# One-layer encoder trunk: the values of all heads projected 512 columns wide in the first stage, and query tiles 0 to 2 as one unit of attention

## The chip, the cores and the metric

The kernel runs on one core of one Trainium2 chip. The metric is the device time of one execution in microseconds (us). Three runs of the kernel before gave 1123.44, 1124.37 and 1125.34 us, so the median is 1124.37 us. All traces are of one profiled execution of that core.

## The reference, cut to what matters

One layer on 1024 tokens of width 1024: RMSNorm and one input projection, whose 2048 columns are 512 of a pooling mixer and 512 each of queries, keys and values; attention of eight heads of 64, where each chunk of 64 tokens sees itself and the eight chunks before it; an output projection; then a gated MLP with a causal convolution, a per-layer embedding and a last norm. The change touches the input projection and the attention alone:

```python
z = hn @ w_in[i]
u = z[..., :POOL_W]
q, k, v = jnp.split(z[..., POOL_W:], 3, axis=-1)
a = pool_mixer(u, pool_w[i], pool_b[i], pool_scale[i])
o = chunk_attention(q, k, v, rel_bias[i])
```

with, for a chunk of queries, `s = q·k * scale + bias`, masked before the first token, `softmax(s)` and `pr·v`.

## The kernel before, in words

**Products.** Everything is computed in float32 with operands split in two: a high half (`hi`, a copy in fp32r made by ScalarE, called ACT here) and a low half (`lo`, the source less `hi`, made by VectorE, called DVE, for some weight blocks by GpSimd, called POOL). `mm3` (L133 to L137) writes one product as three matmuls, hi·hi, hi·lo and lo·hi, so the lines L135, L136 and L137 stand for nearly all of TensorE's (PE's) work. A "product" below is one matmul of these. PE's order is written out by hand; in the attention ACT's and DVE's are too, by `push(t, fn)` with a due time in the unit and `flush()`, which emits what is pending in the order of due times.

**First stage (L230 to L344).** For each of the eight blocks k of the model width, SP loads x in two halves of 512 tokens (L233), the weights of the first pair of query and key heads (L240) and of the values (L237). ACT and DVE weight and split x (L244, L245) and split the weights (`split`, L140 and L141), and square x for the norm (L226, L228). PE multiplies: `start_mm` makes 12 products of 512 columns per k, and `start_v`, one k behind, 9 products of the value columns for the token tiles 0 to 2. Here only the **first four heads' values** are made: 256 columns. `v_tile` makes the same for token tiles 3 to 7, and `v_out` scales and splits the result into `V`.

**Attention (L357 to L751).** A unit is a pair of heads c and one query tile of 128 tokens, except that tiles 0 and 1 make one unit: 7 units for each of 4 pairs, `PER` = 7. `unit(u)` does this in turn: `probs_t(u-1)` transposes the probabilities of the unit before into PSUM (L419); `scores(u)` makes this unit's scores (L396); `ROOM[u % PER]` grants a number of filling steps, each a few products of later projections, drawn from the generator `rest()`; and where a group of query tiles ends, `values` multiplies probabilities and `V` (L471). `softmax` gives DVE the sum with the bias and its minimum (L364, L368), ACT the exponential (L376), DVE the reciprocal (L378), and the scaling of head x = 0 to DVE (L374), of x = 1 to ACT (L372). `probs_out` takes the transposed probabilities out of PSUM as `hi` on ACT (L437) and `lo` on DVE (L439); those past the eighth block of 64 columns lie in other banks and are the "far" ones, with a due time of 3.5 instead of 0.

**Filling.** `rest()` projects the later query, key and mixer columns, 16 steps of three products each per block of 128 columns, and in between (`project_v`, L556) the **other four heads' values**, 256 columns wide, in 32 steps of six products. `weights` and `v_weights` load and split their operands while the block before runs (L502 on ACT, L500 on DVE or POOL); `qk_out` takes a block out of PSUM (L280); `lay` splits it into keys or queries (L309 to L313). `load_bias` loads a head's bias, ACT negates it (L352), POOL writes its two corners (L353, L354). When the units are done, what is left of `rest()` runs beside the output projection.

```python
while credit >= 1:
    if valued[0] and credit < 2 and 4.7 < at[0] < 5.4:
        break
    now[0] += STEP
    credit -= 1
    if next(fill, True) is False:
        break
    lay_due(u)
```

Of the kernel before, what the change touches and what calls it, by code (L numbers as in the profile page):

```python
# [6 lines left out]
F32 = mybir.dt.float32  # L7
# [4 lines left out]
P = 128  # L12
# [52 lines left out]
ROOM = (5.5, 6, 5.5, 6.5, 6.5, 5, 7)  # L65
# [8 lines left out]
UNITS = [(c, ts) for c in range(N_HEADS // 2) for ts in [(0, 1)] + [(t,) for t in range(2, NTOK)]]  # L74
# [26 lines left out]
def trunk(tc, xT, pT, vecs, w_qk0, w_in, w_v, bias, counts, pool_w, w_out, w_up, w_down,  # L101
# [4 lines left out]
    with tc.tile_pool(name="sb", bufs=1) as sb, \  # L106
# [4 lines left out]
        small = sb.tile([P, 88], F32, name="small")  # L111
        R = sb.tile([P, 32768], F32R, name="R")
        F = sb.tile([P, 15488], F32, name="F")
# [56 lines left out]
        biasb = [f(b, 640) for b in (12, 14.5, 57.875)]  # L170
        Sb = [f(b, 640) for b in (17, 19.5)]
# [5 lines left out]
        temps = [f(57.875, 272), f(58.9375, 272)]  # L177
        otmp = f(56.375, 384)
# [16 lines left out]
        wv1 = [r(b, 2048).rearrange("p (k c) -> p k c", k=KT) for b in (128, 136)]  # L195
        VT0 = 3

        def v_mm(t, k, ps, wv):
# [13 lines left out]
        def start_v(k):  # L212
            for t in range(VT0):
                v_mm(t, k, v_ps(t), wv1)
# [15 lines left out]
        for k in range(KT):  # L230
            xs = xraw[k]
            for h in range(2):
# [3 lines left out]
                if k % 2 and h:  # L236
                    sp.dma_start(wvraw[k // 2], w_v[0, :, (k - 1) * 256:(k + 1) * 256])  # L237
# [28 lines left out]
        def v_outs(t, half, ps):  # L266
            s = rstd_tok[:, t:t + 1]
            pv = ps.rearrange("p (h c) -> p h c", h=4)
            hs = slice(4 * half, 4 * half + 4)
            hi, lo = V[:, t, hs, 0:HD], V[:, t, hs, HD:2 * HD]  # L270
            return (lambda: act.activation(hi, pv, AF.Copy, scale=s),
                    lambda: dve.scalar_tensor_tensor(lo, pv, s, rv(hi), ALU.mult, ALU.subtract))

        def v_out(t, half, ps):
            for fn in v_outs(t, half, ps):
                fn()
# [53 lines left out]
        def v_tile(t):  # L330
            for k in range(KT):
                v_mm(t, k, v_ps(t), wv1)

        for t in range(VT0):
            v_out(t, 0, v_ps(t))
        for t in range(VT0, NTOK):
            if t < VT0 + 2:
                rstd_rows(t - VT0)
            v_tile(t)
            v_out(t, 0, v_ps(t))  # L340
# [16 lines left out]
        def softmax(todo, valued):  # L357

            for i, (x, b, ps, S, s_) in enumerate(todo):
# [18 lines left out]
                push(max(2.95 + 0.01 * z, 1.91 + 0.85 * z) if valued else 2.95 + 0.55 * z, lambda s_=s_: dve.reciprocal(s_[:, 2:3], s_[:, 1:2]))  # L378
                push(3.9 + 0.1 * z if x else 3.0 + (0.01 if valued else 0.55) * z, scaled)

        halves = [slice(HD * x, HD * x + HD) for x in range(2)]

        def scores(u):
# [4 lines left out]
            for z, t in enumerate(ts):  # L388
# [3 lines left out]
                places = [[4 + x + 2 * (z + y) for y in range(2 if nk > 3 else 1)] for x in range(2)]  # L392
                for i, (q, k) in enumerate(((Q[0], Kh), (Q[0], Kl), (Q[1], Kh))):
                    for y in range(len(places[0])):
                        for x in range(2):
                            pe.matmul(PS[:, places[x][y], 0:wide], q[halves[x], t * P:(t + 1) * P],  # L396
                                      k[halves[x], ki + y * wide:ki + (y + 1) * wide], start=i == 0, stop=i == 2,
                                      tile_position=(HD * x, 0))
                for x in range(2):
                    p0 = places[x][0]  # L400
                    ps = PS[:, p0:p0 + 3:2, 0:wide] if nk > 3 else PS[:, p0, 0:n]
                    todo.append((x, biasb[(2 * c + x) % 3][:, 640 - n:640], ps, Sb[x][:, z * P:z * P + n],
                                 st[(4 * u + 2 * z + x) % 8]))
            return todo

        def probs_t(u):
# [15 lines left out]
            for t in ts:  # L422
                nk = min(t + 1, BANDT)
                b0 = block_at(t + 1 - nk, t)
                for a, b in ((0, min(nk, 4)), (4, nk)):
# [17 lines left out]
        def values(u):  # L443
# [6 lines left out]
            while c_ >= 2 and len(v_ready) < t1 or u < NU - 1 and at[0] < 2.3:  # L450
# [32 lines left out]
        blocks_, ready = [8 + 1, 4 + 1, 8 + 2, 4 + 2, 8 + 3, None, 4 + 3, 2, 3, 0, 1], {}  # L483

        wvr, wv2, there = [], [], set()
# [9 lines left out]
        def split_later(parts, soon=False):  # L495

            t = now[0] - 0.3 if soon else max(5.2, now[0] + 0.4)
            for i, (name, src, hi, lo) in enumerate(parts):
# [3 lines left out]
                push(t + 0.7 * i * (not soon), lambda src=src, hi=hi: act.activation(hi, src, AF.Copy))  # L502
                push(t + (0.25 + 0.02 * i if soon else 0.8 + 0.7 * i), low)

        def v_weights(z):
            wv2.append([w[0] for w in (slot(), slot())] if z == 0 else [slot()[0], r(156, 1024).rearrange("p (k c) -> p k c", k=4)])
            split_later([(("v", z, k), wvr[z][:, k], wv2[z][0][:, k], wv2[z][1][:, k])
                         for k in (slice(0, 2), slice(2, 4))], z == 1)

        def v_load(z):  # L510
            wvr.append(load(w_v[1, :, z * 1024:(z + 1) * 1024]).rearrange("p (k c) -> p k c", k=4))

        def weights(ct, half):
# [7 lines left out]
            split_later([((ct, half), raws_[ct][:, 4 * half:4 * half + 4], hi, lo)], ct == 4 + 3)  # L521
# [3 lines left out]
        def project(ct, evac, wait=None):  # L525
# [4 lines left out]
            for h in range(2):  # L530
# [4 lines left out]
                for k in range(KT):  # L535
# [6 lines left out]
                    if (h, k) == ((1, 0) if behind == blocks_[-1] else (0, 2)) and behind != "":  # L542
                        v_load(0) if behind is None else weights(behind, 0)
                    if (h, k) == (0, 5) and behind is None:
                        v_load(1)
                    if (h, k) == (1, 4) and behind != "":
                        v_weights(0) if behind is None else weights(behind, 1)
# [8 lines left out]
        def project_v():  # L556
            assert 2 * PER - 1 <= unit_at[0] < 2 * PER + 1
            v_weights(1)
            flush()
            for t0 in range(0, NTOK, 2):  # L560
                bankn[0] += 1
                bank = bankn[0] % 2
                if bank in owed:
                    flush()
                order = [(t, z) for t in (t0, t0 + 1) for z in range(2)]
                if t0 in (0, NTOK - 2):
                    order[1:3] = order[2:0:-1]
                for i, (t, z) in enumerate(order):
                    ps = PS[:, bank, 256 * (t % 2):256 * (t % 2) + 256]
                    if (t0, i) == (NTOK - 2, 2):  # L570
                        weights(4 + 3, 0)
                        weights(4 + 3, 1)
                    for k in range(4 * z, 4 * z + 4):
                        mm3(ps, XTH[t // 4][:, k, t % 4 * P:(t % 4 + 1) * P],
                            XTL[t // 4][:, k, t % 4 * P:(t % 4 + 1) * P], wv2[z][0][:, k % 4], wv2[z][1][:, k % 4],
                            i == 0 and k == 0, k == KT - 1, True)
                        if k % 2:
                            at[0] = 1.44 * i + 0.36 * (k % 4 + 1)
                            yield True
                for z in range(2):  # L580
                    t = t0 + z
# [925 lines left out]
```

## Time and profile before

| | |
|---|---|
| runs | 1123.44, 1124.37, 1125.34 us (median 1124.37) |
| the profiled execution | 1124.14 us, of which the span of the trace is 1122.3 us |
| granted TensorE clock, mean | 0.998 |
| PE busy | 1112.2 us (99%) in 5866 matmuls |
| weight loads (PEld) | 932.0 us (83%) |
| DVE, ACT, POOL busy | 853.5, 583.7, 166.7 us |
| first stage, 0 to 54.4 us | PE busy 52.62 us |
| attention, 54.4 to 253.6 us | PE busy 197.29, DVE 137.16, ACT 133.43 us of 199.20 |
| transfers, 54.4 to 253.6 us | 37 GB/s |

Matmuls overlap in the records, since they are pipelined: a 512-column product reads as 390 ns long though the next begins sooner. How long a product holds PE is therefore read from one start to the next, and a stall is read as a start that comes later than that.

### The profile page before, as it was taken

How to read it: one execution, taken by the hardware profiler on the slowest of the kernel's cores; microseconds unless marked ns; L12 is line 12 of the kernel's file. 1: busy time of each engine (PE TensorE's matmuls, PEld its weight loads, DVE VectorE, ACT ScalarE, POOL GpSimd, SP SyncE). 2: the span in 40 equal slices, each digit the busy share in tenths (PEclk: the TensorE clock that was granted, in tenths of full speed). 3: DMA queues.
4: the chain of work that ended last, by engine and by line, in shares of the span. 5: the costliest groups of instructions: out<-in, count | busy, mean ns of one | idle time of the engine just before them, and what ended most of it. 6: DMA issues, size and time to landing. Idle time of an engine off the chain costs nothing.

```text
span 1122.3 us, 16025 instructions
## 1 busy us (share of the span) xinstructions
PE 1112.2 (99%) x5866; PEld 932.0 (83%) x5866; DVE 853.5 (76%) x1442; ACT 583.7 (52%) x1010; POOL 166.7 (15%) x212
## 2 busy tenths in 40 slices
PE   9999999999999999999999999999999999999997
PEld 7978799888888888888888888888888888888887
DVE  7466676678668878878787878787877789986845
ACT  8366676665664544444443435343444444664634
POOL 0012000186003200210122011201120112000000
PEclk9999999999999999999999999999999999999999
DMA  8101020204610352674667455756575556430003
GB/s 282 38 20 62 20 63 19 61 19 132 196 35 5 99 161 87 159 170 133 159 152 171 138 160 142 175 144 155 144 170 151 132 154 132 147 94 20 1 26 124
DMA packets 64591, 124.86 MB, mean 111 GB/s; under 512 B 7296, under 2 KB 8704, under 8 KB 64512
## 3 DMA queue, kind: packets, MB, share of 16 engines
q1 hardware_dynamic: 50400, 98.33, 27.0%
q0 software_dynamic: 13824, 25.17, 14.0%
q8 instruction: 46, 0.75, 0.3%
q10 hardware_dynamic: 288, 0.33, 0.1%
q14 instruction: 33, 0.27, 0.1%
HBM read 109.13 MB, written 14.68 MB: 110 GB/s over the span
## 4 chain that ended last, share of the span: by engine, by line
PE 89%; DVE 4%; issue 3%; ACT 2%; POOL 1%; DMA 0%; POOLq 0%; SPq 0%; DVEq 0%; ACTq 0%
PE PS L135 28%; PE PS L136 28%; PE PS L137 27%; PE PS L471 2%; PE PS L396 2%; PE PS L419 1%; DVE R L141 1%; DVE B L439 1%; ACT F L376 1%; ACT R L140 1%; DMA F<-in_xT 0%; POOL TB L966 0%; PE PS L819 0%; DVE F L948 0%; DVE F L1232 0%
## 5 line engine op out<-in xcount | busy, mean ns | idle before, releaser
L135 PE MATMUL PS<-R 128*128 128x512 f32 (+1 forms) x1152 | 441.2, 383 | 0.1
L137 PE MATMUL PS<-R 128*128 128x512 f32 (+1 forms) x1152 | 437.2, 380 | 0.0
L136 PE MATMUL PS<-R 128*128 128x512 f32 (+1 forms) x1088 | 419.3, 385 | 0.3 <-DVE R L245 0.3
L135 PEld LDWEIGHTS PS<-R 128*128 128x128 f32 x1152 | 216.9, 188 | 45.0 <-issue 2.5
L137 PEld LDWEIGHTS PS<-R 128*128 128x128 f32 x1152 | 216.8, 188 | 40.9
L136 PEld LDWEIGHTS PS<-R 128*128 128x128 f32 x1088 | 204.7, 188 | 40.5 <-DVE R L245 1.1
L140 ACT ACTIVATE R<-F 128x512 fp32r<-128x512 f32 (+2 forms) x221 | 137.3, 636 | 176.4 <-PE PS L136 77.1
L141 DVE TENSOR_TENSOR R<-F,R 128x512 fp32r<-128x512 f32 (+2 forms) x221 | 154.2, 712 | 49.3 <-ACT R L140 48.8
L891 DVE TENSOR_TENSOR F<-F 128x512 f32<-128x512 f32 x88 | 60.5, 688 | 49.5 <-DMA F<-in_w_up 45.9
L1201 DVE TENSOR_TENSOR F<-F,PS 128x512 f32<-128x512 f32 x140 | 92.5, 682 | 5.9 <-PE PS L137 5.8
L140 ACT ACTIVATE BQ<-RW 128x512 fp32r<-128x512 f32 x90 | 52.6, 622 | 78.6 <-PE PS L136 74.6
L1144 POOL DMA_DIRECT2D RW<-Yd x56 | 49.2, 879 | 266.9 <-DMA RW<-Yd 202.8
L1144 POOL DMA_DIRECT2D RW<-in_w_down x40 | 36.1, 951 | 225.0 <-DMA RW<-in_w_down 190.6
L141 DVE TENSOR_TENSOR BQ<-RW,BQ 128x512 fp32r<-128x512 f32 x90 | 59.1, 686 | 1.8 <-PE PS L136 1.3
L136 PE MATMUL PS<-BQ 128*128 128x512 f32 x140 | 54.7, 390 | 0.1
L137 PE MATMUL PS<-R,BQ 128*128 128x512 f32 x140 | 54.6, 390 | 0.0
L135 PE MATMUL PS<-R,BQ 128*128 128x512 f32 x140 | 54.6, 390 | 0.0
L135 PE MATMUL PS<-BQ 128*128 128x512 f32 x140 | 54.5, 389 | 0.0
L137 PE MATMUL PS<-BQ 128*128 128x512 f32 x140 | 54.5, 389 | 0.0
L136 PE MATMUL PS<-R,BQ 128*128 128x512 f32 x140 | 54.5, 389 | 0.0
L376 ACT ACTIVATE F<-F,small 128x640 f32<-128x640 f32 (+4 forms) x64 | 44.0, 689 | 18.5 <-DVE small L364 15.5
L1027 ACT ACTIVATE F<-F,vec 128x1024 f32<-128x1024 f32 (+1 forms) x25 | 28.6, 1143 | 47.3 <-DVE F L1002 42.5
(178 smaller groups left out, 1605.4 us busy)
## 6 DMA issues: line engine op xcount, KB each, us to landing
F<-in_w_up SPq DMA_DIRECT2D x91, 256.0 KB, 4.3
RW<-Yd SPq DMA_DIRECT2D x60, 256.0 KB, 3.9
RW<-Yd POOLq DMA_DIRECT2D x56, 256.0 KB, 5.0
RW<-in_w_down SPq DMA_DIRECT2D x50, 256.0 KB, 2.9
RW<-in_w_down POOLq DMA_DIRECT2D x40, 256.0 KB, 6.3
Yd<-F SPq DMA_DIRECT2D x40, 256.0 KB, 2.8
F<-in_w_in SPq DMA_DIRECT2D x10, 512.0 KB, 3.5
F<-in_xT SPq DMA_DIRECT2D x16, 256.0 KB, 5.7
```

The lines of the kernel that those rows point to most:

```text
L135: pe.matmul(ps, ahi, bhi, start=first, stop=False, skip_group_check=more)
L136: pe.matmul(ps, ahi, blo, start=False, stop=False, skip_group_check=more)
L137: pe.matmul(ps, alo, bhi, start=False, stop=last, skip_group_check=more)
L140: both = (act.activation(hi, src, AF.Copy), dve.tensor_tensor(lo, src, rv(hi), ALU.subtract))
L141: dve.tensor_tensor(lo, src, rv(hi), ALU.subtract))
L376: push(1.9 + 0.85 * z, lambda S=S, s_=s_: act.activation(S, S, AF.Exp, bias=s_[:, 0:1], scale=-1.0, accum_out=s_[:, 1:2]))
L396: pe.matmul(PS[:, places[x][y], 0:wide], q[halves[x], t * P:(t + 1) * P], k[halves[x], ki + y * wide:ki + (y + 1) * wide], start=i == 0, s ...
L471: pe.matmul(Os[j][:, (a - t0) * P:(b - t0) * P].rearrange("p (t q) -> p t q", q=P), V[:, k, 2 * c_ + j], PT[part][:, b0:b0 + by * (b - a - ...
L891: return dve.tensor_tensor(rawu[to], rawu[a], rawu[b], op)
L1027: act.activation(y, Gb[:, 2 + a:2 + b], AF.Identity, bias=vec[:, C_CB + fi:C_CB + fi + 1], scale=cw(2))
L1144: pool.dma_start(t, src, accum_op=ALU.add)
L1201: dve.tensor_tensor(t, t, PS[:, 4 + d], ALU.subtract if n in (1, 5) else ALU.add)
```

## The change

**Values.** The weights `w_v` are stored 512 columns wide, and a block of them is loaded and split in the first stage for every k (before, 256 columns, two k at a time). `start_v` and `v_tile` make 512-column products for all eight heads. `project_v`, `v_weights`, `v_load` and the wait for `v_ready` are gone. Loads move in SP's order: one `w_v` block now stands between the first and the second block of x.

**Units.** Tiles 0, 1 and 2 are one unit, so there are 6 per pair of heads, 24 in all where there were 28. The scores of tiles 0 and 1 share PSUM banks 4 and 5 (columns 0 and 256 on), and those of tile 2 lie in banks 6 and 7; before, tile 1 had 6 and 7. The map buffers `Sb` grow to 768 columns, and some buffers move in SBUF.

**Filling.** `ROOM` is dealt anew, from 42 steps per pair to 34, and queries of the next pair are laid out from the second unit on rather than the third.

```diff
-ROOM = (5.5, 6, 5.5, 6.5, 6.5, 5, 7)
+ROOM = (5, 5, 6.5, 6.5, 4.5, 6.5)
...
-UNITS = [(c, ts) for c in range(N_HEADS // 2) for ts in [(0, 1)] + [(t,) for t in range(2, NTOK)]]
+UNITS = [(c, ts) for c in range(N_HEADS // 2) for ts in [(0, 1, 2)] + [(t,) for t in range(3, NTOK)]]
...
-        wv1 = [r(b, 2048).rearrange("p (k c) -> p k c", k=KT) for b in (128, 136)]
+        wv = [r(b, 4096).rearrange("p (k c) -> p k c", k=KT) for b in (128, 144)]
...
         def v_ps(t):
-            return PS[:, (4, 5, 6, 4, 5, 6, 7, 3)[t], 0:256]
+            return PS[:, (4, 5, 6, 4, 5, 6, 7, 3)[t]]
...
-                if k % 2 and h:
-                    sp.dma_start(wvraw[k // 2], w_v[0, :, (k - 1) * 256:(k + 1) * 256])
+                if h:
+                    sp.dma_start(wvraw[k % 4], w_v[:, k * 512:(k + 1) * 512])
...
-            if k % 2:
-                wv = wvraw[k // 2].rearrange("p (k c) -> p k c", k=2)
-                split(wv, wv1[0][:, k - 1:k + 1], wv1[1][:, k - 1:k + 1])
+            split(wvraw[k % 4], wv[0][:, k], wv[1][:, k])
...
-                places = [[4 + x + 2 * (z + y) for y in range(2 if nk > 3 else 1)] for x in range(2)]
+                off, place = (0, 1, 3)[z] * P, ((0, 0), (0, 256), (1, 0))[z]
+                places = [[4 + x + 2 * (place[0] + y) for y in range(2 if nk > 3 else 1)] for x in range(2)]
...
-                return (2, HD * n) if n < 8 else (6, 384 + HD * (n - 8))
+                return (2, HD * n) if n < 8 else (6, 512 + HD * (n - 2 * total))
...
-            while c_ >= 2 and len(v_ready) < t1 or u < NU - 1 and at[0] < 2.3:
+            while u < NU - 1 and at[0] < 2.3:
...
-            yield from project_qk(3, (1,))
-            yield from project_v()
-            yield from project_qk(3, (0,))
+            yield from project_qk(3)
...
-                if u >= (c - 1) * PER + (0 if x else PER - 1 if h else 2):
+                if u >= (c - 1) * PER + (0 if x else PER - 1 if h else 1):
...
-    d["w_v"] = c(w_in[:, 1536:].reshape(KT, P, 2, 256).transpose(2, 1, 0, 3)).reshape(2, P, KT * 256)
+    d["w_v"] = c(w_in[:, 1536:].reshape(KT, P, 512).transpose(1, 0, 2)).reshape(P, KT * 512)
```

How the filling products stand in the order that PE gets: before, the 28 units hold 12 to 27 products of 512 columns each, or up to 42 of 256 where the values are made; in the change, the first pair's six units hold 15, 21, 15, 21, 12 and 21, the second pair's 12, 18, 18, 21, 12 and 21, the third's 21, 9, 21, 21, 21 and 15, the fourth's 15, 18, 18, 21, 12 and 21. 27 follow the last unit and 273 the last values, in both kernels.

The order of ACT's work at the start, before: x (L244, 512 tokens each), the weights of queries and keys (L140, 256 columns), the square of x (L226) and the weights of values (L140 into B).

```order
L244 ACTIVATE R<-F,vec 128x512
L140 ACTIVATE R<-F 128x256
L244 ACTIVATE R<-F,vec 128x512
L140 ACTIVATE R<-F 128x256
L244 ACTIVATE R<-F,vec 128x512
L226 ACTIVATE F<-F 128x1024
L244 ACTIVATE R<-F,vec 128x512
L140 ACTIVATE B<-F 128x512
```

And in the change:

```order
L244 ACTIVATE R<-F,vec 128x512
L140 ACTIVATE R<-F 128x256
L244 ACTIVATE R<-F,vec 128x512
L140 ACTIVATE B<-F 128x512
L140 ACTIVATE R<-F 128x256
L226 ACTIVATE F<-F 128x1024
L244 ACTIVATE R<-F,vec 128x512 x2
L140 ACTIVATE B<-F 128x512
```

A value block's `hi` and the square of the first x block now stand ahead of the first half of the second x block.

ACT's order where the first pair of heads gives way to the second, before: the end of the last unit (L372), a query half laid out (L312), a bias negated (L352), the probabilities out of PSUM (L437), and the exponentials (L376) of tiles 0 and 1.

```order
L372 ACTIVATE F<-F,small 128x640
L312 ACTIVATE R<-F 128x512
L352 ACTIVATE F<-F 128x640
L437 ACTIVATE B<-PS 128x1024
L376 ACTIVATE F,small<-F,small 128x128 x2
L376 ACTIVATE F,small<-F,small 128x256 x2
L437 ACTIVATE B<-PS 128x256
L372 ACTIVATE F<-F,small 128x128
L372 ACTIVATE F<-F,small 128x256
```

And in the change, where the same lines have the numbers L365, L305, L345, L433 and L369, and L498 is a weight block's `hi` (L502 before):

```order
L365 ACTIVATE F<-F,small 128x640
L305 ACTIVATE R<-F 128x512
L498 ACTIVATE B<-F 128x512
L498 ACTIVATE R<-F 128x512
L345 ACTIVATE F<-F 128x640
L433 ACTIVATE B<-PS 128x1024
L369 ACTIVATE F,small<-F,small 128x128 x2
L369 ACTIVATE F,small<-F,small 128x256 x2
L369 ACTIVATE F,small<-F,small 128x384 x2
L433 ACTIVATE B<-PS 128x256
L365 ACTIVATE F<-F,small 128x128
L365 ACTIVATE F<-F,small 128x256
```

Two weight blocks now stand ahead of the probabilities, and two more exponentials ahead of the far ones (the L433 of 256 columns).

## Rows read from the trace of the kernel before

**Rows 1.** The page, busy time of each engine (share of the span, instructions).
```profile
PE 1112.2 (99%) x5866; PEld 932.0 (83%) x5866; DVE 853.5 (76%) x1442; ACT 583.7 (52%) x1010; POOL 166.7 (15%) x212
```
**Rows 2.** Busy time by stretch: us of each engine, granted clock, DMA share, GB/s.
```profile
54.40:253.60 199.20, 197.29 (x1623) 167.98 (x1621) 137.16 (x341) 133.43 (x277) 40.41 (x61) 1.00 0.12 37
```
**Rows 3.** Timeline of PE (start, us, engine, line): 41 narrow products, then 37 wide.
```profile
175.57 0.28 PE L136 MATMUL PS<-B,R 128*128 128x256 f32 x1
...
180.35 0.28 PE L137 MATMUL PS<-R 128*128 128x256 f32 x1
...
331.71 0.39 PE L136 MATMUL PS<-R 128*128 128x512 f32 x1
...
339.89 0.39 PE L136 MATMUL PS<-R 128*128 128x512 f32 x1
```
**Rows 4.** Timeline of the start: the second block of x on ACT, DVE and PE.
```profile
7.74 0.73 ACT L244 ACTIVATE R<-F,vec 128x512 fp32r<-128x512 f32 x1 [0.34 <-DMA F<-in_xT]
...
8.37 1.04 ACT L226 ACTIVATE F<-F 128x1024 f32<-128x1024 f32 x1
...
10.05 0.75 DVE L245 SCALAR_TENSOR_TENSOR R<-F,vec,R 128x512 fp32r<-128x512 f32 x1 [0.81 <-ACT R L244]
...
10.60 0.39 PE L135 MATMUL PS<-R 128*128 128x512 f32 x1
```
**Rows 5.** Busy time by stretch, as in rows 2, at the start.
```profile
6.00:7.50 1.50, 1.50 (x6) 0.84 (x5) 0.38 (x1) 1.03 (x2) 0.00 (x0) 1.00 0.82 261
```
**Rows 6.** Timeline of PE: one unit of tile 2, 18 products between its scores and 217.50.
```profile
212.00 0.59 PE L419 MATMUL PS<-ident,F 64*128 64x64 f32 x12
212.40 0.77 PE L396 MATMUL PS<-R 64*128 64x384 f32 x6
...
217.50 0.59 PE L419 MATMUL PS<-ident,F 64*128 64x64 f32 x12
```
**Rows 7.** What PE waited for, 50 to 256 us: us in total, times, longest.
```profile
PE PS L419 <- DVE B L439: 1.7, 4, 0.8
```
**Rows 8.** Timeline of PE: two of these waits, in brackets, before transposes.
```profile
79.54 0.84 PE L419 MATMUL PS<-ident,F 64*128 64x64 f32 x20 [0.39 <-DVE B L439]
...
116.60 0.40 PE L419 MATMUL PS<-ident,F 64*128 64x64 f32 x6 [0.76 <-DVE B L439]
```
**Rows 9.** Timeline of the unit of tiles 0 and 1, fourth pair; its transposes begin at 203.49.
```profile
203.49 0.84 PE L419 MATMUL PS<-ident,F 64*128 64x64 f32 x20
...
204.17 0.63 ACT L312 ACTIVATE R<-F 128x512 fp32r<-128x512 f32 x1 [1.22 <-DVE F L280]
204.71 0.61 ACT L502 ACTIVATE R<-F 128x512 fp32r<-128x512 f32 x1
...
205.23 0.73 ACT L352 ACTIVATE F<-F 128x640 f32<-128x640 f32 x1
205.40 1.30 POOL L500 TENSOR_TENSOR R<-F,R 128x512 fp32r<-128x512 f32 x1 [10.42 <-ACT R L502]
...
205.86 1.00 ACT L437 ACTIVATE B<-PS 128x1024 fp32r<-128x1024 f32 x1
...
206.82 0.29 DVE L368 CUSTOM_DVE_ANT_0 F<-PS,F 128x128 f32<-128x128 f32 x1 [1.08 <-POOL F L353]
...
208.54 0.36 ACT L437 ACTIVATE B<-PS 128x256 fp32r<-128x256 f32 x1
208.59 3.48 PE L471 MATMUL PS<-B,R 128*128 128x256 f32 x24
```
**Rows 10.** Timeline of the first unit: the last scalings on ACT, the next transposes.
```profile
57.74 0.83 ACT L372 ACTIVATE F<-F,small 128x128 f32<-128x128 f32 x2
...
59.21 0.59 PE L419 MATMUL PS<-ident,F 64*128 64x64 f32 x12
```
**Rows 11.** Timeline of tile 3's unit, second pair: scores, and `lo` of tile 2 on DVE.
```profile
117.00 0.95 PE L396 MATMUL PS<-R 64*128 64x256 f32 x12
...
119.82 0.95 DVE L439 TENSOR_TENSOR B<-PS,B 128x768 fp32r<-128x768 f32 x1
```

More of the change, by code (lines that the diff above doesn't have):

```diff
@@ L169, in trunk @@
         rstd_bc = f(8, 1024)
-        biasb = [f(b, 640) for b in (12, 14.5, 57.875)]
-        Sb = [f(b, 640) for b in (17, 19.5)]
+        biasb = [f(b, 640) for b in (18, 56.375, 58.875)]
+        Sb = [f(b, 768) for b in (12, 15)]
         o32 = f(22, 4096).rearrange("p (h t) -> p h t", h=4)
@@ L264, in trunk, with v_out @@
         start_v(KT - 1)
-        def v_outs(t, half, ps):
+        def v_out(t, ps):
             s = rstd_tok[:, t:t + 1]
[L268 to L276, printed above, removed]
+            pv = ps.rearrange("p (h c) -> p h c", h=N_HEADS)
+            hi, lo = V[:, t, :, 0:HD], V[:, t, :, HD:2 * HD]
+            act.activation(hi, pv, AF.Copy, scale=s)
+            dve.scalar_tensor_tensor(lo, pv, s, rv(hi), ALU.mult, ALU.subtract)
         def qk_out(c, h, ps):
@@ L339, in trunk @@
             v_tile(t)
-            v_out(t, 0, v_ps(t))
+            v_out(t, v_ps(t))
         for h in range(2):
@@ L395, in scores @@
                         for x in range(2):
-                            pe.matmul(PS[:, places[x][y], 0:wide], q[halves[x], t * P:(t + 1) * P],
+                            pe.matmul(PS[:, places[x][y], place[1]:place[1] + wide], q[halves[x], t * P:(t + 1) * P],
                                       k[halves[x], ki + y * wide:ki + (y + 1) * wide], start=i == 0, stop=i == 2,
@@ L424, in probs_t @@
                 b0 = block_at(t + 1 - nk, t)
-                for a, b in ((0, min(nk, 4)), (4, nk)):
+                for a, b in ((0, min(nk, 4 - m)), (max(4 - m, 0), nk)):
                     if b > a:
@@ L481, in trunk @@
         at = [0]
-        blocks_, ready = [8 + 1, 4 + 1, 8 + 2, 4 + 2, 8 + 3, None, 4 + 3, 2, 3, 0, 1], {}
-        wvr, wv2, there = [], [], set()
+        blocks_, ready = [8 + 1, 4 + 1, 8 + 2, 4 + 2, 8 + 3, 4 + 3, 2, 3, 0, 1], {}
+        there = set()
         def slot(last=None):
@@ L493, in slot, with split_later @@
             return wring[(nw[0] - 1) % 3]
-        def split_later(parts, soon=False):
-            t = now[0] - 0.3 if soon else max(5.2, now[0] + 0.4)
+        def split_later(parts):
+            t = max(5.2, now[0] + 0.4)
             for i, (name, src, hi, lo) in enumerate(parts):
@@ L501, in low @@
                     there.add(name)
[L502 to L511, printed above, removed]
+                push(t + 0.7 * i, lambda src=src, hi=hi: act.activation(hi, src, AF.Copy))
+                push(t + 0.8 + 0.7 * i, low)
         def weights(ct, half):
@@ L542, in project @@
                     if (h, k) == ((1, 0) if behind == blocks_[-1] else (0, 2)) and behind != "":
-                        v_load(0) if behind is None else weights(behind, 0)
-                    if (h, k) == (0, 5) and behind is None:
-                        v_load(1)
+                        weights(behind, 0)
                     if (h, k) == (1, 4) and behind != "":
-                        v_weights(0) if behind is None else weights(behind, 1)
+                        weights(behind, 1)
                     at[0] = 0.68 * (k + 1)
@@ L554, in project, with project_qk @@
                 owed.add(bank)
[L556 to L581, printed above, removed]
-                    hi, lo = v_outs(t, 1, PS[:, bank, 256 * z:256 * z + 256])
-                    push(now[0], hi)
-                    push(now[0] + 0.5, lo)
-                    v_ready.append(t)
-                owed.add(bank)
-            assert unit_at[0] < 2 * PER + 5
-        def project_qk(p, xs=(1, 0)):
-            for x in xs:
+        def project_qk(p):
+            for x in (1, 0):
                 def evac(h, ps, x=x):
```

34 lines of the change are left out of this document (18 added, 16 removed).

## The prediction

> **What bounds the kernel now.** First the page: PE is busy 99% of the span, DVE 76%, ACT 52% [rows 1]. That is read as "PE has hardly a gap", not as "PE runs at its peak", because the records of pipelined matmuls overlap. So I went on to the timeline of PE and took starts, not durations. From the first start to the last of 37 wide products there are 36 steps in 8.18 us, 227 ns each; 41 narrow ones make 40 steps in 4.78 us, 120 ns each [rows 3]. A stretch that consists of such steps is bound by the number of products; any larger step is a stall. Second the attention by stretch: in its 199.2 us DVE is busy 137.2 us and ACT 133.4 us [rows 2], so neither bounds it on average, but each is at two thirds, and a unit is only as fast as the chain of its softmax. Third PE's waits: 1.7 us in four waits by the view [rows 7], the longest 0.76 us [rows 8]. They stand before transposes, where a `lo` half of the last probabilities still has to leave PSUM. Start-to-start gaps show three smaller ones that the pipelined records cover; I put all waits of the attention at 2.5 us. The reader is to see that PE's own work sets the end nearly everywhere, so the change is worth what it saves PE, less the waits it makes.
>
> **The change part by part.** The sum is made against the profiled execution, 1124.14 us with a span of 1122.3 us; the median of the three runs is 0.23 us above it.
>
> *Wide values.* 8 token tiles x 8 blocks x 3 matmuls x 2 halves are 384 narrow products at 120 ns, 46.1 us; 192 wide ones at 227 ns are 43.6 us: **-2.5 us** [rows 3]. All of it is on PE's path. The moves do not add to it: 23 us of filling leave the attention, and 21 us enter the first stage.
>
> The pair shows that a narrow product costs 6 ns more than half a wide one. The Trainium skill (TensorE: Matmul & The Clock Gate, section "Wait — 56ns, not 53.3ns?") says of this that a warm matmul costs its columns at 2.4 GHz plus some 2.5 ns; by that, two narrow ones cost only 2.5 ns more than a wide one, 192 of these are 0.5 us, and the sum below would come out 2 us higher. The row disagrees with it, 240 against 227 ns, and the rows decide.
>
> *ACT, DVE and SP in the first stage.* Splits and evacuations become twice as wide; each `v_tile` gives PE 24 x 227 ns = 5.4 us, ample cover for two evacuations. Cover is missing at the very start. Before, the second block's second half is ready just in time: its low half is made on DVE from 10.05 for 0.75 us, and the products that use that half begin at 10.60 [rows 4]. Now 256 KB of value weights land ahead of it, at 261 GB/s [rows 5] 1.0 us, and on ACT their `hi` (0.6 us) and the square of 1.04 us stand ahead of the first half's L244, which began at 7.74, while the square followed it at 8.37 [rows 4]. By hand: value weights landed at 7.3, their `hi` to 7.95, query weights to 8.35, square to 9.3, L244 twice to 10.65, low halves on DVE to 11.45; the second half's products begin at 11.95 rather than 10.60: **+1.3 us**. If the extra transfer hides behind the start-up of the queue, 0.6; if it costs its full second and one split more, 1.6. From the third block on PE has 21 x 227 ns = 4.8 us of work per block, and ACT and DVE need about 3.8 us each, so nothing more is lost.
>
> *One unit less per pair.* A tile-2 unit takes 5.50 us from its transposes to the next ones; its 18 products are 4.09 us, so 1.41 us are transposes, scores and switching [rows 6]. Within a larger unit the 12 transposes add 0.25 to 0.4 us and the 6 scores (0.70 us to the next product, switching included) 0.55. The difference is 0.5 us per pair, four times: **-2.0 us** (-1.6 to -2.4).
>
> *Waits in the attention.* The work of ACT and DVE stays, less 8 evacuations and 4 splits, but the attention has some 25 us less of PE's work beside it. So I went through the units by hand, with the orders of ACT, DVE and POOL and the durations of the rows.
>
> - The first unit has 15 products again, but six maps rather than four. Before, the scalings on ACT ended at 58.57 and the transposes began at 59.21 [rows 10]; two more exponentials (0.6 us each, an estimate from the 0.83 us of the scalings of 128 and 256 columns) and a scaling (0.6) make ACT end 1.8 us later, and the last value tile leaves PSUM half a us later: **+0.8**, since the scores of tile 2 give PE 0.6 us and the transposes come in turn.
> - The unit where the second pair begins is the worst. From its transposes: a query half on ACT at 0.05, two weight splits and the negated bias to 2.4, the probabilities to 3.4. POOL makes two low halves of 1.25 us each before it writes the bias corners, at 3.9; DVE waits for these, as at 206.82 [rows 9]. The six exponentials then end at 6.9 and the far probabilities at 7.3. PE has 0.65 us of transposes, 1.6 of scores and 12 products, so it begins the values at 5.0 and needs the far halves after three matmuls: 1.9 us for `hi`, 0.5 for `lo`: **+2.4**. In the unit of rows 9 one split less and one exponential pair less had the far `hi` at 208.54, when the values began.
> - Tile 3 of the third pair has 9 products. In the second pair `lo` of tile 2 left PSUM 2.8 to 3.8 us after the first scores [rows 11]; now it is a far half and comes after the scaling, at 4.5, with 2.9 us of PE's work before the values: two waits, **+1.1**.
> - Tile 4 of the first pair keeps its 15 products and so its wait of 0.4 [rows 8]; tile 7 of the third has 15 too, 0.4; two units more 0.2 to 0.35. Together **+1.3**.
>
> These are 5.6 us against the 2.5 that go with the old units: **+3.1 us**.
>
> Sum: -2.5 + 1.3 - 2.0 + 3.1 = -0.1 us, and so **1124.0 us**: no change. What the attention's end hands on (273 products after the last values) is the same.
>
> **The rivals.**
>
> *ACT and POOL keep up (faster).* The waits depend on what stands in the queues at a pair's end, and by hand I may have placed a split or an evacuation too late. If the second pair's unit waits 0.5 us and tile 3 not at all, the waits are at their old size: -2.5 + 1.3 - 2.0 = -3.2, **1120.9 us**; with the start at 0.6, 1120.2. For it speaks that ACT and DVE are at two thirds on average; against it, that the unit of rows 9 had its far half ready only as the values began.
>
> *Every pair change queues like the second (slower).* The merged unit begins with the splits and the bias of the pair before it in ACT's and POOL's queues. I gave the third and fourth pair no wait there, since 21 and 15 products cover it and part of that work is already done. If both wait like the second, 2 x 2.4 us more: **1128.8 us**; at half of it, 1126.4. It decides from 2.25 us more than my 5.6, which is one such unit. For it speaks that the six exponentials take 3 us of ACT in each; against it, the products.
>
> *The narrow product was not dearer.* If the 13 ns come from what stands around the products and not from their width, the first term goes to -0.5: 1126.0 us. The 40 steps were read in an undisturbed run of filling, so I give it little.
>
> **How the numbers follow.** About 0.2%, 2.25 us, is what a measurement of this kernel can tell from no change. My forecast, -0.1, with its terms within their bounds, stays within that: 0.40. The first rival, 0.34, is the faster side: many estimates of mine put a wait where a reordering would hide it. The second, with the third where it adds to waits, 0.26. The range reaches from the first rival's best case to between the second rival's half and full price: 1120.0 to 1128.0; less than 2 in 10 lie outside.
>
> **What would show it right or wrong.** In PE's timeline: 192 value products with steps of 227 ns in the first stage and none of 256 columns before the tail; the products of the second block's second half near 12 us, and the first scores near 76 us, 22 us later than the 54.6 of before; 24 units; a gap of about 2 us inside the second pair's first values; no gap at the third and fourth pair's. It is wrong if the values of the second pair follow without a gap (then the first rival), if gaps of 2 us stand at all three pair changes (the second), or if the gaps are as said and the end still moves, which would put it after the attention, where I see nothing changed.

## The result, and the profile after

| | before | changed |
|---|---|---|
| median of 7 runs, us | 1124.23 | 1128.46 (1126.98 to 1132.06) |
| ratio to before, 95% interval | | 1.0039, 1.0026 to 1.0052 |
| profiled execution, us | 1124.14 | 1128.46 |
| its span, us | 1122.3 | 1126.7 |
| PE, first scores to the end of the last values, us | 54.63 to 262.76 | 76.03 to 266.21 |
| filling products in between | 447 wide, 192 narrow | 447 wide |

The change makes the kernel slower by 0.4%; the forecast was no change, and the time lies just above its range. First the page's busy times, then the view by stretch (columns as in [rows 2]) from the first scores to the last values:

```profile
PE 1112.3 (99%) x5674; PEld 922.9 (82%) x5674; DVE 850.0 (75%) x1438; ACT 581.9 (52%) x1006; POOL 165.3 (15%) x212
```

```profile
76.03:266.21 190.18, 184.99 (x1480) 153.76 (x1480) 135.91 (x340) 130.43 (x274) 50.70 (x76) 0.99 0.14 43
```

The same stretch of the kernel before:

```profile
54.63:262.76 208.13, 206.22 (x1672) 175.87 (x1672) 143.06 (x348) 136.05 (x282) 49.10 (x73) 1.00 0.14 45
```

PE did nothing for 5.2 us of this stretch (190.18 - 184.99), against 1.9 before (208.13 - 206.22), although the page still says 99%: over the whole span 3 us don't show in whole per cents. The granted clock fell too, to 0.99 on average. DVE and ACT lost only 7.2 and 5.6 us of work while PE lost 21.2.

One number serves from here on: **PE's rest**, the length of this stretch less its filling at 227 ns per wide and 120 ns per narrow product [rows 3]. It holds scores, transposes, values, switching and every wait. Before: 208.13 - 447 x 0.227 - 192 x 0.120 = 83.6 us; after: 190.18 - 101.5 = **88.7 us**. The span's 4.4 us then divide so: the first scores come 21.40 us later where 23.04 us of filling moved ahead of them, so -1.64, which is -2.5 for the widths and +0.9 for the start; the rest +5.1; the last values to the last product 853.5 against 853.1, +0.4; and the stretch behind the last product +0.5.

What PE waited for in the attention (as [rows 7], here 54 to 264 us):

```profile
PE PS L467 <- ACT B L433: 2.2, 2, 1.8
PE PS L467 <- DVE B L435: 1.1, 3, 0.5
PE PS L415 <- DVE B L435: 0.8, 2, 0.4
PE PS L137 <- DVE B L496: 0.7, 1, 0.7
PE PS L467 <- DVE F L273: 0.3, 1, 0.3
PE PS L415 <- ACT F L365: 0.2, 1, 0.2
```

The largest stands where the second pair begins. PE's timeline there, then DVE's and POOL's:

```profile
122.68 0.51 PE L467 MATMUL PS<-B,R 128*128 128x256 f32 x3
124.97 0.96 PE L467 MATMUL PS<-B,R 128*128 128x128 f32 x6 [1.79 <-ACT B L433]
126.40 3.17 PE L467 MATMUL PS<-B,R 128*128 128x128 f32 x15 [0.46 <-DVE B L435]
129.50 1.28 PE L415 MATMUL PS<-ident,F 64*128 64x64 f32 x24
...
119.61 0.08 DVE L361 DVE_READ_ACCUMULATOR2_ANT small<- 128x1 f32 x1
121.64 0.29 DVE L361 CUSTOM_DVE_ANT_0 F<-PS,F 128x128 f32<-128x128 f32 x1 [1.95 <-POOL F L346]
...
118.99 1.29 POOL L496 TENSOR_TENSOR B<-F,B 128x512 fp32r<-128x512 f32 x1 [16.02 <-ACT B L498]
120.24 1.28 POOL L496 TENSOR_TENSOR R<-F,R 128x512 fp32r<-128x512 f32 x1
121.46 0.15 POOL L346 MEMSET F<- 64x64 f32 x1
```

POOL fills the bias corners only after two weight low halves, DVE's second reduction waits 1.95 us for that, the softmax ends late, and PE stands with three value products done. What follows was in no term of the prediction: from 126.40 on, 15 value products take 3.1 us to the transposes, and these 1.1 to the next scores. By stretch of 2 us:

```profile
124.00:126.00 2.00, 0.96 (x6) 0.76 (x6) 1.96 (x11) 1.69 (x6) 0.00 (x0) 1.00 0.00 0
126.00:128.00 2.00, 1.60 (x9) 1.60 (x10) 0.34 (x2) 0.61 (x1) 0.00 (x0) 0.72 0.00 0
128.00:130.00 2.00, 2.00 (x18) 1.78 (x18) 0.00 (x0) 0.38 (x1) 0.00 (x0) 0.50 0.03 8
130.00:132.00 2.00, 2.00 (x34) 1.82 (x32) 1.25 (x3) 1.52 (x4) 0.00 (x0) 0.92 0.00 0
```

PE is busy all through 128 to 130, but at a granted clock of 0.50: 1.2 GHz, after it had stood.

### The profile page after: what moved, and what is told of

Same layout as the page of the kernel before. It is cut to its first block, busy times and chain, and to the rows that moved or that the text cites. A ratio compares the mean times of both kernels' runs of the same rounds, so it can differ in the third digit from the quotient of the medians.

```text
span 1126.7 us, 15615 instructions
## 1 busy us (share of the span) xinstructions
PE 1112.3 (99%) x5674; PEld 922.9 (82%) x5674; DVE 850.0 (75%) x1438; ACT 581.9 (52%) x1006; POOL 165.3 (15%) x212
## 4 chain that ended last, share of the span: by engine, by line
PE 64%; DVE 3%; issue 2%; ACT 1%; POOL 1%; POOLq 0%; DVEq 0%; ACTq 0%
PE PS L135 21%; PE PS L136 21%; PE PS L137 21%; DVE R L141 1%; ACT R L140 1%; POOL TB L917 0%; POOL F L907 0%; DVE F L899 0%; DVE F L1183 0%; ACT TB L888 0%; PE PS L770 0%; POOL small L774 0%; ACT F L762 0%; DVE TB L910 0%; DVE TB L911 0%
## 5 line engine op out<-in xcount | busy, mean ns | idle before, releaser
L135 PE MATMUL PS<-R 128*128 128x512 f32 (+1 forms) x1088 | 422.5, 388 | 0.6 <-ACT R L244 0.5
L136 PE MATMUL PS<-R 128*128 128x512 f32 (+1 forms) x1088 | 419.0, 385 | 0.3 <-DVE R L245 0.3
L137 PE MATMUL PS<-R 128*128 128x512 f32 (+1 forms) x1088 | 418.8, 385 | 0.0
L135 PEld LDWEIGHTS PS<-R 128*128 128x128 f32 x1088 | 204.7, 188 | 45.5 <-issue 2.7
L137 PEld LDWEIGHTS PS<-R 128*128 128x128 f32 x1088 | 204.7, 188 | 41.1 <-DVE R L141 0.2
L136 PEld LDWEIGHTS PS<-R 128*128 128x128 f32 x1088 | 204.8, 188 | 40.5 <-DVE R L245 0.8
L140 ACT ACTIVATE R<-F 128x512 fp32r<-128x512 f32 (+2 forms) x221 | 137.3, 636 | 173.1 <-PE PS L136 83.0
L1152 DVE TENSOR_TENSOR F<-F,PS 128x512 f32<-128x512 f32 x140 | 92.6, 681 | 5.8 <-PE PS L137 5.6
L140 ACT ACTIVATE BQ<-RW 128x512 fp32r<-128x512 f32 x90 | 52.6, 622 | 79.5 <-PE PS L136 75.4
L369 ACT ACTIVATE F<-F,small 128x640 f32<-128x640 f32 (+4 forms) x64 | 43.9, 688 | 14.7 <-DVE small L357 12.6
```

Of the source, the lines that this page charges most:

```text
L135: pe.matmul(ps, ahi, bhi, start=first, stop=False, skip_group_check=more)
L136: pe.matmul(ps, ahi, blo, start=False, stop=False, skip_group_check=more)
L137: pe.matmul(ps, alo, bhi, start=False, stop=last, skip_group_check=more)
L140: both = (act.activation(hi, src, AF.Copy), dve.tensor_tensor(lo, src, rv(hi), ALU.subtract))
L369: push(1.9 + 0.85 * z, lambda S=S, s_=s_: act.activation(S, S, AF.Exp, bias=s_[:, 0:1], scale=-1.0, accum_out=s_[:, 1:2]))
L1152: dve.tensor_tensor(t, t, PS[:, 4 + d], ALU.subtract if n in (1, 5) else ALU.add)
```

## The experiments

Each kernel was timed beside the kernel before on the same chip; the ratio is to that. Columns: median; ratio with its interval; PE's rest, worked out as above; PE's idle time in the same stretch (length less PE busy). Rest and idle time are of one profiled execution of each kernel, the times of several.

| kernel | us | ratio | rest | idle |
|---|---|---|---|---|
| before | 1124.2 | | 83.6 | 1.9 |
| the change | 1128.5 | 1.0039 (1.0026 to 1.0052) | 88.7 | 5.2 |
| wide values alone | 1132.7 | 1.0073 (1.0061 to 1.0086) | 92.6 | 8.9 |
| merged units alone | 1119.8 | 0.9962 (0.9949 to 0.9976) | 79.4 | 0.3 |
| change, bias early | 1124.5 | 1.0000 (0.9991 to 1.0009) | 84.8 | 3.0 |
| change, PE kept busy | 1126.2 | 1.0016 (1.0008 to 1.0025) | 86.9 | 2.6 |
| change, thicker filling | 1147.3 | 1.0199 (1.0185 to 1.0213) | 80.7 | 0.8 |
| change, start | 1126.1 | 1.0015 (1.0006 to 1.0024) | 89.9 | 4.9 |
| change, bias and start | 1123.7 | 0.9996 (0.9988 to 1.0005) | 85.0 | 3.2 |
| before, dealt anew | 1124.5 | 1.0003 (0.9995 to 1.0012) | 84.0 | 2.8 |
| change, bias, flat dealing | 1129.7 | 1.0042 (1.0029 to 1.0054) | 84.6 | 2.9 |
| the same and the start | 1127.5 | 1.0027 (1.0018 to 1.0036) | 84.6 | 2.8 |
| bias, flat dealing, longer last unit | 1129.6 | 1.0047 (1.0033 to 1.0061) | 84.5 | 2.8 |
| the same and the start | 1128.1 | 1.0036 (1.0024 to 1.0049) | 84.6 | 2.8 |

The filling taken off is 447 wide products (and 192 narrow ones where they are still there), except that the wide values alone have 441 in this stretch, the merged units alone 459, the thicker filling 552, and the first two kernels with flat dealing 429. The ten products that keep PE busy are not taken off: they are 2.3 us of that kernel's rest.

### The two halves of the change by themselves

Wide values, with the old units:

```diff
-ROOM = (5, 5, 6.5, 6.5, 4.5, 6.5)
+ROOM = (4.5, 4.5, 4.5, 5.5, 5.5, 4, 5.5)
-UNITS = [(c, ts) for c in range(N_HEADS // 2) for ts in [(0, 1, 2)] + [(t,) for t in range(3, NTOK)]]
+UNITS = [(c, ts) for c in range(N_HEADS // 2) for ts in [(0, 1)] + [(t,) for t in range(2, NTOK)]]
```

> The changed kernel with the old division into 28 units (tiles 0 and 1 together, tile 2 by itself, each tile's scores in banks of its own) and its wide value projection; filling steps per pair 34 as in the change, dealt over seven units. Theory A (the loss is the second pair's merged unit: the bias corners stand on POOL behind two weight low halves, DVE waits 1.95 us for them, PE stands 2.6 us and then runs 3.5 us at half clock): without merged units the widths alone give -2.5 on PE, +0.9 at the start and about as many waits as before, so 1122 to 1124 us and no half clock inside the attention. Theory B (the loss is the thinner filling: 23 us less of products beside the attention, so every unit waits, whatever its division): 1127 us or more, with waits spread over many units.

It took 1132.7 us, 8.3 more than before and more than the whole change: theory B's side. The waits stand in every pair (the view by stretch, then PE's waits):

```profile
75.71:268.43 192.72, 183.83 (x1474) 151.59 (x1474) 135.37 (x336) 131.39 (x270) 50.29 (x75) 1.00 0.13 42
```

```profile
PE PS L415 <- DVE B L435: 7.8, 13, 1.1
PE PS L467 <- ACT B L433: 0.5, 1, 0.5
PE PS L467 <- DVE B L435: 0.3, 1, 0.3
```

Thirteen waits of transposes for the low half of the last probabilities. Ahead of these transposes the step from the last filling product is too long by 0.9 to 1.2 us where a one-tile unit without values has 12 products, by 0.1 to 1.1 with 15, by 0.1 to 0.5 with 18; with 21, as in the change, it is too long by 0.1 everywhere, which I take for the switch itself. Only this one dealing of the 34 steps over seven units was run.

Merged units, with the old values as filling:

```diff
-ROOM = (5.5, 6, 5.5, 6.5, 6.5, 5, 7)
+ROOM = (6.5, 6, 8, 8, 5.5, 8)
-UNITS = [(c, ts) for c in range(N_HEADS // 2) for ts in [(0, 1)] + [(t,) for t in range(2, NTOK)]]
+UNITS = [(c, ts) for c in range(N_HEADS // 2) for ts in [(0, 1, 2)] + [(t,) for t in range(3, NTOK)]]
```

> The kernel before with tiles 0, 1 and 2 as one unit and nothing else: values of the second four heads still fill the attention (42 filling steps per pair, dealt over six units; the second pair's merged unit has 27 products in place of the change's 12). Theory A: the same queues stand there, but 27 products (6.1 us) cover the softmax, so PE has no stall of 2 us, the clock stays at 1.00, and the fewer units give 1.4 to 2.0 us: 1122.2 to 1123 us. Theory B expects the same, since filling is plenty. Theory C (a merged unit costs by itself what it saves, through six maps in one softmax and tiles 0 and 1 in one bank): 1124 us or more.

It took 1119.8 us, less than any other kernel here and 2.4 us below the best that was expected. PE is idle for 0.3 us (by stretch, then a row of PE's timeline):

```profile
54.18:260.84 206.66, 206.39 (x1684) 177.68 (x1684) 145.93 (x357) 137.98 (x291) 54.15 (x78) 1.00 0.14 46
```

```profile
108.00 2.96 PE L474 MATMUL PS<-B,R 128*128 128x256 f32 x24
```

The second row is the unit in which the change stands for over 2 us: here 27 products come ahead of its 24 values, which run through. The two ratios multiply to 0.9962 x 1.0073 = 1.0035, the change's 1.0039 within its interval: the halves add, and the merged units give back half of what the wide values cost.

### Is it the cover?

Cover is PE's independent work that runs while ACT, DVE and POOL make what PE needs next. The next kernel adds 105 products to the filling of the attention:

```diff
-                    mm3(PS[:, bank], hi[:, k % 4], lo[:, k % 4], XTH[h][:, k], XTL[h][:, k], k == 0, k == KT - 1)
+                    if k % 3 != 2 and unit_at[0] < NU:
+                        mm3(PS[:, bank], hi[:, k % 4], lo[:, k % 4], XTH[h][:, k], XTL[h][:, k], k == 0, False)
+                        pe.matmul(PS[:, bank], hi[:, k % 4], XTH[h][:, k], start=False, stop=k == KT - 1)
+                    else:
+                        mm3(PS[:, bank], hi[:, k % 4], lo[:, k % 4], XTH[h][:, k], XTL[h][:, k], k == 0, k == KT - 1)
```

> The changed kernel with 105 extra wide products among the filling of its units, one in each of six of a half's eight steps, so that the attention is again as thick with PE's work as before the change (23.8 us at 227 ns); their result is added to the projections of pairs 1 to 3 and of the pooling branch, which are therefore not the reference's. Theory D (what the change lost is cover: the waits come from the 23 us of filling that left the attention): PE's time in the units besides the filling falls from 88.7 us to 82 or 83, so the kernel takes 1146 to 1147 us, 5.5 to 6.5 us less than the added work. Rival (the waits have other causes, in the new units or in the queues, and do not shrink under more products): 1152 us.

The rest falls further than expected, to 205.97 - (447 + 105) x 0.227 = 80.7 us, and PE is idle for 0.8:

```profile
76.04:282.01 205.97, 205.15 (x1586) 172.09 (x1585) 135.58 (x341) 131.76 (x276) 51.17 (x77) 1.00 0.12 40
```

In the attention 23.8 us of added work cost 15.8. The median, 1147.3 us, is a little over what was expected, although the rest fell further: from the last values to the end the kernel takes 3.6 us more than the change, with a wait of PE of 1.7 us for ACT among them, which I did not follow up. So theory D holds for the attention: once they are covered, the new units and queues leave PE idle for 0.8 us, less than the 1.9 of before.

### The second pair's stall, and the clock behind it

```diff
+        def turns_first(c):
+            return 2 * c + 3 < N_HEADS
...
                             push(3.0, lambda h=h: turns.append(load_bias(h)))
+                    if turns_first(c):
+                        push(4.6, lambda: turns.pop(0)())
...
-            if turns and (u % PER == PER - 1 or u % PER == 1):
+            if turns and u % PER == 1:
```

> The changed kernel with one thing moved: the negated bias and its two corner fills for the next pair's second head are issued at the end of tile 7's softmax, ahead of the query half and the weight splits, instead of behind them. Theory A: DVE's first reductions of that unit no longer wait for POOL; they start near 119.9 rather than 121.6, PE's stall in the second pair's values goes from 2.6 to about 1 us, the clock stays at 1.00 there (1.4 us more), so 3 to 3.5 us less than the changed kernel: 1125.0 to 1125.5 us. Theory B: only that one wait goes and others take its place: 1127.5 to 1128.5 us.

It took 1124.5 us, 4.0 less than the change and 0.5 below the range that was expected. The corners now lie ahead of POOL's low halves, DVE goes on at once, one wait of 0.42 is left in these values, and the clock stays at 1.00 throughout the attention (the rows: POOL, DVE, PE, and PE by stretch):

```profile
118.04 0.14 POOL L346 MEMSET F<- 64x64 f32 x1 [14.67 <-ACT F L345]
...
119.46 1.30 POOL L496 TENSOR_TENSOR B<-F,B 128x512 fp32r<-128x512 f32 x1 [1.08 <-PE PS L415]
...
120.04 0.29 DVE L361 CUSTOM_DVE_ANT_0 F<-PS,F 128x128 f32<-128x128 f32 x1
...
124.03 2.77 PE L467 MATMUL PS<-B,R 128*128 128x128 f32 x21 [0.42 <-ACT B L433]
126.74 0.97 PE L415 MATMUL PS<-ident,F 64*128 64x64 f32 x24
...
128.00:130.00 2.00, 2.00 (x15) 1.61 (x14) 1.96 (x7) 1.52 (x6) 0.00 (x0) 1.00 0.00 0
```

To separate the stall from the clock, the next kernel keeps PE busy in the stall with products that nothing reads, and moves nothing in the other queues:

```diff
+                    for _ in range({(0, 3): 8, (0, 9): 2}.get((j, n_), 0) if u == 5 else 0):
+                        pe.matmul(PS[:, 4], XTH[0][:, 0, 0:P], XTH[0][:, 0], start=True, stop=True)
```

> The changed kernel with ten extra products of 512 columns that nothing reads, put into the second pair's values where PE stands (8 before the fourth value product, 2 before the tenth); the waits for the far halves stay as they are. If the half clock after the stall comes from PE's idleness there, the granted clock stays at 1.00 in 125 to 131 us, the waits are unchanged, and the time falls by what the half clock costs, 1.4 us: 1127.0 us, with less spread between runs. If the half clock comes for another reason, it stays, and the time is 1128.5 us, or up to 0.3 us more for products that outlast the wait.

It took 1126.2 us. From the transposes ahead of the stall (117.76 in the change, 117.99 here) to those of tile 3 the two units take 18.20 us rather than 19.67 with the same filling, **1.5 us** less, and the clock by stretch is full:

```profile
126.00:128.00 2.00, 2.00 (x16) 1.57 (x14) 0.58 (x3) 0.62 (x1) 0.00 (x0) 1.00 0.03 8
128.00:130.00 2.00, 2.00 (x40) 1.86 (x40) 0.49 (x2) 1.27 (x4) 0.00 (x0) 1.00 0.00 0
```

The medians differ by more, 2.3 us. The profiled execution is one of several: the change's seven runs have mean granted clocks from 0.993 (1132.06 us) to 0.998 (1126.98 us), so the half clock probably costs some of them more than the profile shows. The profile of the kernel in the next section shows such a case: the same stall, then nearly 7 us at 0.50:

```profile
124.00:126.00 2.00, 1.79 (x10) 1.50 (x10) 1.08 (x5) 1.08 (x3) 0.00 (x0) 0.57 0.00 0
126.00:128.00 2.00, 2.00 (x11) 2.00 (x11) 0.00 (x0) 0.00 (x0) 0.00 (x0) 0.50 0.00 0
128.00:130.00 2.00, 2.00 (x30) 1.77 (x29) 0.42 (x1) 0.76 (x2) 0.00 (x0) 0.50 0.04 8
```

### The start

```diff
-                if h:
-                    sp.dma_start(wvraw[k % 4], w_v[:, k * 512:(k + 1) * 512])
+                for j in () if not h or k == 0 else (0, 1) if k == 1 else (k,):
+                    sp.dma_start(wvraw[j % 4], w_v[:, j * 512:(j + 1) * 512])
...
-            split(wvraw[k % 4], wv[0][:, k], wv[1][:, k])
+            for j in () if k == 0 else (0, 1) if k == 1 else (k,):
+                split(wvraw[j % 4], wv[0][:, j], wv[1][:, j])
```

> The changed kernel with the first value weights loaded and split one block later (behind the second block of x and its splits, as a pair with the second value weights). By the terms of the prediction the start is then as before the change: PE's waits at 8 to 11 us fall from 1.3 to 0.6 us or less, and the kernel takes 0.7 to 1.3 us less: 1127.2 to 1127.8 us. Rival: the transfer is late anyway and the wait moves to the third block: no change, 1128.5 us.

The first scores come at 74.76 rather than 76.03, 1.3 us earlier, as the first theory says. The median falls by 2.4, to 1126.1, below the 1127.2 to 1127.8 that were expected; the interval of that difference reaches down to about 1, and I make no more of it. The rest is higher than the change's, 89.9 against 88.7, because of the longer stretch at half clock just shown. The product that waits for the second x block's first low half begins at 10.60 in the change and at 9.11 here (the change's two waits, then this kernel's one):

```profile
9.81 0.50 PE L135 MATMUL PS<-R 128*128 128x512 f32 x1 [0.55 <-ACT R L244]
10.60 0.50 PE L136 MATMUL PS<-R 128*128 128x512 f32 x1 [0.28 <-DVE R L245]
```

```profile
9.11 0.50 PE L136 MATMUL PS<-R 128*128 128x512 f32 x1 [0.29 <-DVE R L245]
```

> The changed kernel with both repairs, the bias early and the first value weights one block later, and the change's own dealing. They touch different places, so they should add: 1124.5 less 1.0 to 1.5 us, 1123.0 to 1123.5 us, a little faster than the kernel before, with PE's units besides the filling at 84.8 us as with the bias early alone. Rival (both gains were partly the half clock, which only one can remove): 1124 to 1124.5 us.

It took 1123.7 us: both repairs together bring the change level with the kernel before, no further; its rest is 85.0 where the merged units alone have 79.4.

### Can the thin filling be dealt better?

```diff
-ROOM = (5.5, 6, 5.5, 6.5, 6.5, 5, 7)
+ROOM = (5.5, 5, 6, 7, 6.5, 5, 7)
```

> The kernel before, its 42 filling steps per pair dealt otherwise (5.5, 5, 6, 7, 6.5, 5, 7 in place of 5.5, 6, 5.5, 6.5, 6.5, 5, 7), so that its two longest waits, before the fifth unit's and the tenth unit's transposes, have 21 to 24 and 18 products in place of 15 and 12. Nothing else. If the 4.6 us of the merged units alone are partly this dealing (their units besides the filling fell by 4.2 us, of which some 2 are the fewer transposes, scores and switches, and some 2 are waits), the waits of 2.4 us fall to about 1 and the kernel takes 1122.5 to 1123.3 us. Rival (merging alone took the waits away): 1124.0 to 1124.7 us.

It took 1124.5 us, no gain. The two waits went, and four others of 0.6 to 1.3 us came, ahead of the transposes at 150.6, 165.1, 202.7 and 217 us. So this dealing alone is not what the merged units gained by.

The change with the bias early, dealt flat:

```diff
-ROOM = (5, 5, 6.5, 6.5, 4.5, 6.5)
+ROOMS = (5, 7, 6, 6, 5, 6, 4, 5, 6, 6, 5, 5, 6, 4.5, 6, 6, 5, 6, 5, 5, 6, 7, 5, 7)
```

> The changed kernel with the bias issued early (as in the experiment on the bias) and the same amount of filling dealt flatter: 18 products for single tiles, 15 to 18 where values stand, 12 to 15 for the merged units and 15 for tile 3 of the third pair in place of 9. The runs so far show that a unit of one tile waits 1.2 us with 12 products, 0.46 with 15 and nothing with 18. Theory E (the thin filling could be dealt without waits): PE's time in the units besides the filling goes from 84.8 to about 82 us, and the kernel to 1121.5 to 1122.5 us. Rival (every product moved opens a wait where it is taken from): 1124.0 to 1125.0 us.

> The last kernel with the first value weights one block later as well. If the parts add: 0.7 to 1.3 us below it, 1120.3 to 1121.5 us, which would be faster than the kernel before; against the merged units alone (1119.8 us) it has 2.5 us less of value products and some 2.5 us more of waits. Rival: the start gives nothing: 1121.5 to 1122.5 us.

They took 1129.7 and 1127.5 us. The rest stays at 84.6, against 84.8 with the change's dealing, and 3 us are lost behind the attention. These two kernels leave 18 products more to run there, behind the loads of the output weights, and part of the mixer's channels is not the reference's. With `DRAIN = 15` in place of 9 these products run in the last unit:

> The flatter dealing of the seventh experiment again, but with the 18 products that it had left over for after the attention put into the last unit, ahead of its values (45 in place of 27), so that the output weights no longer overtake the last projection. The units besides the filling stand at 84.6 us as there (84.8 with the change's dealing): if the thin filling is what sets the waits, the dealing changes nothing and the kernel takes 1124 to 1125 us, as with the bias early alone. Rival (the dealing was good and the gap of 3 us behind the attention hid it): 1121.5 to 1122.5 us.

> The last kernel with the first value weights one block later: 1.0 to 1.5 us below it. With the theory that the dealing changes nothing, 1123 to 1123.5 us, so that no repair of the change reaches the merged units alone (1119.8 us). Rival: 1120.5 to 1121.5 us.

They took 1129.6 and 1128.1 us; all four lie 4.6 to 5.0 us above what even the slower theory had. The rest is the same, 84.5 and 84.6, so this flatter dealing moved the waits and removed next to nothing of their sum. The time is lost behind the attention, which neither theory had: the last mixer columns are projected later, POOL pools them until 282.4 (269.4 with the change's dealing), PE waits for the mixing, and its clock falls (POOL, PE, and by stretch):

```profile
281.46 0.91 POOL L581 TENSOR_TENSOR F<-F 128x254 f32<-128x254 f32 x1
...
284.18 0.50 PE L135 MATMUL PS<-B 128*128 128x512 f32 x1 [3.17 <-ACT F L596]
...
286.00:288.00 2.00, 2.00 (x6) 1.57 (x5) 1.90 (x6) 1.70 (x3) 0.00 (x0) 0.50 0.33 111
```

## Why the prediction was wrong

**Waits in the attention, +3.1: the term that failed.** It was to hold the cover that leaves with the filling, unit by unit and by hand, and it was less than half of what was lost. Put together from units of each shape that run without a wait, the change's rest would be 79.2 us (an estimate; the merged units alone have 79.4), so its waits are 88.7 - 79.2 = 9.5; before, they were 83.6 - 79.2 - 2.0 = 2.4, where 2.0 is what the merging itself saves. That is +7.1 where the forecast had +3.1. One by one: the second pair's stall 2.8 (2.4 forecast, and by the very queue: two low halves on POOL ahead of the bias corners); tile 3 of the third pair 1.3 (1.1); the first unit 0.6 (0.8); the smaller ones 2.4 (1.3). Two had no term at all: the half clock behind the stall, 1.5, and the last unit's wait for a weight low half (L496), 1.0.

**Wide values, -2.5: right as a count.** The last 96 value products of the first stage make 95 steps in 21.65 us, 228 ns each, where before they made them in 11.47, 121 ns each (the first and the last of them, before and then in the change):

```profile
42.95 0.36 PE L135 MATMUL PS<-B,R 128*128 128x256 f32 x1
...
54.42 0.28 PE L137 MATMUL PS<-B,R 128*128 128x256 f32 x1
```

```profile
54.07 0.48 PE L135 MATMUL PS<-B,R 128*128 128x512 f32 x1
...
75.72 0.39 PE L137 MATMUL PS<-B,R 128*128 128x512 f32 x1
```

The sentence behind that term, "The moves do not add to it: 23 us of filling leave the attention, and 21 us enter the first stage", holds for PE's work and not for the time. Those 23 us were cover. Without them the attention's rest grows by 9.0 us (92.6 against 83.6) in the kernel with the wide values alone; as many products put back take the change's rest from 88.7 to 80.7.

**Start, +1.3: near enough**, 0.9 in the profile, 1.3 by the experiment. ACT's queue ran as forecast, and the second block's second half begins at 11.86 (11.95 forecast); the waits stand before its first half, 0.55 and 0.28 us. **Fewer units, -2.0: right.** From tile 7's transposes through the filling behind the next pair's tile 4 the units take 10.4 us besides the filling where nothing waits, in the kernel with the merged units alone, against 10.9 before: 0.5 per pair. With filling enough to cover it, merging is worth 4.2 us of the rest, since the waits of before go too.

No term of the forecast lay behind the attention, where 0.9 us were lost.

**What was to show it.** The 192 narrow products gone from the attention, first scores near 76 (76.03), the gap of about 2 us in the second pair's first values, two waits in the third pair's tile 3: as written. At the third and fourth pair's change, where I saw no gap, there are 0.5 and 0.2. The last sign, "the end still moves, which would put it after the attention", is not where most of it went: 0.9 us of the 4.4 lie there.

**The rivals.** "Every pair change queues like the second" gave nearly the time, 1128.8, by another mechanism: the other changes hardly waited, so it is luck that its number comes close. "ACT and POOL keep up" is out, since the second pair's values and tile 3 of the third waited; "The narrow product was not dearer" is out by the steps above. None of the rivals had the cover itself, or the clock.

## What to carry to other kernels

Filling is worth its time twice: as work, and as cover for the chain beside it. Before moving it out, add up what each stretch then has left against the chain it hid: here a one-tile unit wanted 18 to 21 products, and taking nearly a fifth of the filling away cost 9 us in the dealing that was tried, more than three times what doing it in wider pieces saved. A change in two halves is worth measuring by halves: the merged units alone, at 1119.8 us, are 0.4% faster than the kernel before and 0.8% faster than the change.

## What the runs showed of the hardware

A stall of PE can be paid twice. After PE had stood 1.79 and 0.46 us, with six value products in between, it ran at a granted clock of 0.50 (1.2 GHz) for some 3 us in which it was busy, which cost 1.5 us more in this profile; ten products that nothing reads, run in the stall, kept the clock at 1.00 and made the kernel 2.3 us faster. The same kernel's seven runs differ by 5 us; the slowest has the lowest mean clock.

It is not always so. With the flat dealing PE stood 2.91 us in one piece behind the attention, longer than that stall, and the clock stayed at 1.00 (PE, then by stretch); with the longer last unit a wait of 3.17 us was followed by 0.50. What decides it is not shown here.

```profile
267.23 0.50 PE L135 MATMUL PS<-R,B 128*128 128x512 f32 x1 [2.91 <-DVE F L553]
...
268.00:270.00 2.00, 2.00 (x10) 1.64 (x9) 0.00 (x0) 1.06 (x1) 0.73 (x2) 1.00 0.00 0
270.00:272.00 2.00, 2.00 (x11) 1.65 (x10) 0.00 (x0) 0.00 (x0) 0.00 (x0) 1.00 0.00 0
```
